# Top-k of four heads at a time, and the last gathered sum transposed later

## The chip, the cores and the metric

The kernel runs on one core of a Trainium2 chip. The time is device microseconds from the first to the last instruction of one launch, with what the launch adds around it; runs of the kernel before gave 2964.22 us in the median (2958.63 to 2974.24, three runs). The profile is of one more execution.

## The reference, cut to what matters

Two transformer blocks on 256 tokens of width 2048. The change concerns the end of the second: an expert layer with product keys, and a gate behind it.

```python
def peer(xn, w_pq, sub_k1, sub_k2, expert_u, expert_v):      # 8 heads, 128 keys a half, top 16
    q = (xn @ w_pq).reshape(B, S, 8, 2, 128)
    s1 = jnp.einsum('bshd,hnd->bshn', q[..., 0, :], sub_k1)
    s2 = jnp.einsum('bshd,hnd->bshn', q[..., 1, :], sub_k2)
    v1, i1 = lax.top_k(s1, 16)
    v2, i2 = lax.top_k(s2, 16)
    cand = (v1[..., :, None] + v2[..., None, :]).reshape(B, S, 8, 256)
    vs, ci = lax.top_k(cand, 16)
    e1 = jnp.take_along_axis(i1, ci // 16, axis=-1)
    e2 = jnp.take_along_axis(i2, ci % 16, axis=-1)
    eidx = e1 * 128 + e2                                      # one of 16384 experts
    gates = jax.nn.softmax(vs, axis=-1)
    # per token: act = gelu(expert_u[eidx] . xn);  out = sum of act * gates * expert_v[eidx]

h = h + peer(rms_norm_2(h, ffn_norm_gain), ...)
gate = jax.nn.sigmoid(rms_norm_2(h, ple_norm_gain) @ w_ple_gate)
h = h + gate * (p @ w_ple_proj)
```

## The kernel before

The program is written out by hand: each engine executes its instructions in the order in which the Python code issues them. A main line issues the projections, weight chunk by weight chunk (128 rows by 1024 numbers, 0.5 MB, four raw buffers, loaded by SyncE). Beside it run generators in *lanes*: at each new chunk `next_chunk` calls `lanes.step()`, and every lane, from lane 0 upward, goes on to its next `yield`. `until(name)` steps the lanes until a flag is set. So a generator's delay is a count of steps, not of time, and an instruction that waits holds up all that is behind it on its engine.

The expert layer has these parts.

- **Query projection** `project1`: 32 chunks of `w_pq`, 16 columns; after every second block `beside()` steps the lanes of the top-k and of the gathers once. `pq_done` copies a column from PSUM on ScalarE (L1544), `score` multiplies by the keys (L1553) and scales on ScalarE (L1555). Two columns make the scores of one head.
- **Top-k** `topk`: two lanes, even and odd heads. Per head, on two token tiles of 128: the 16 best of 128 for both halves (`top16`, L1572 to L1583), 256 candidate sums on GpSimd (L1601), the 16 best of these, the position split into two digits by six GpSimd instructions (L1606 to L1611), a comparison with 0..15 (L1616), four products on GpSimd (L1618), a sum (L1624), and the expert index on GpSimd (L1626 to L1628). The softmax of the 16 values is done in the head as well: negated maximum on GpSimd (L1612), exponential on ScalarE (L1620), reciprocal (L1625), scale (L1633).
- **First gather** `u_rows`: 256 slots (two token tiles by 128), for each an indirect DMA of one row of `w_u` per token (L1663, 128 rows of 8 KB, issued by GpSimd) and one product with sum on VectorE (L1703). Ten seats hold gathered rows for the first 128 slots, four for the rest. A seat comes free when its product is issued, and the gather waits for that product. Products begin when four heads have indices; while fewer than eight have, a product is issued every third step.
- **Weights and spots**: `weights` makes gelu times gate after products 127 and 255; `spots` builds one-hot matrices and from them, on TensorE, dense weight planes `G`.
- **Second half**: the first 1024 columns of the expert output come from 128 chunks of `w_vd` multiplied with `G` (the loop at L1878, 8 blocks a chunk, L1900), the other 1024 from 256 gathers of `w_vs` with weighted sums on VectorE (`v_rows`, L1840), two a chunk. When a tile's sum is complete it is copied (L1847) and `turned` transposes it on TensorE (L1815) and adds it to `x`: eight steps later for tile 0, at once for tile 1.
- **Gate**: after the loop the sums are added to `x` (L1904), `x_block` splits blocks 0 to 7 into high and low parts (L545, L546) and squares them for the norm (L563, L564); a narrow projection by `w_pp` follows (2 blocks deep, 16 columns, L1912), then `until("v")`, blocks 8 to 15, the norm `n5` and the gate projection of 32 chunks of `w_pg`, whose first blocks are those of rows 0 to 1023. Every chunk of `w_pp` and `w_pg` is split into a high part on ScalarE (L349) and a low part on VectorE (L350), two chunks ahead.

Of the kernel before, what the change touches and what calls it, by code (L numbers as in the profile page):

```python
# [63 lines left out]
def layout(i):  # L64
# [50 lines left out]
    a["w_pg"] = blocks(i["w_ple_gate_2"][0])  # L115
# [110 lines left out]
def program(tc, A, out, stage=99, dbg=None):  # L226
# [129 lines left out]
    lanes = Lanes(5)  # L356
    flags = {}

    def until(name):
        while not flags.get(name):  # L360
            lanes.step()
# [1169 lines left out]
    subk, qring, eg, ek, kk = cK(8, 2, 128), cK(4, T), cK(2, 128), cK(8, 2, 2, 16), cK(2, 128)  # L1531
    G.dma_start(subk.rearrange("p h s n -> p (h s n)"), A["subk"])
    sc = slab("sc").rearrange("p (t h s n) -> p t h s n", t=2, h=8, s=2)
    cT = Carve("cT")
# [51 lines left out]
    def topk(first):  # L1586

        cand, oh = cT(2, 16, 16), cT(2, 2, 16, 16)
        vv, ii, iif = cT(2, 2, 16), cT(2, 2, 16).bitcast(U32), cT(2, 2, 16)
        vs, ci, cf, c1, gs = cT(2, 16), cT(2, 16).bitcast(U32), cT(2, 16), cT(2, 2, 16), cT(2, 4)  # L1590
        xf = cT(2, 16)
        flat = lambda v: v.rearrange("p t s n -> p (t s n)")
        for h in range(first, 8, 2):
            while flags.get(("sc", h), 0) < 2:
                yield
            hs = slice(h * 16, h * 16 + 16)
            both = [(tt, s) for tt in range(2) for s in range(2)]
            yield from top16([(sc[:, tt, h, s], vv[:, tt, s], ii[:, tt, s]) for tt, s in both])
            G.tensor_copy(iif, ii)
            for tt in range(2):  # L1600
                G.tensor_add(cand[:, tt], vv[:, tt, 0][:, :, None].to_broadcast([128, 16, 16]),  # L1601
                             vv[:, tt, 1][:, None, :].to_broadcast([128, 16, 16]))
            yield
            yield from top16([(cand[:, tt].rearrange("p a b -> p (a b)"), vs[:, tt], ci[:, tt]) for tt in range(2)])

            G.tensor_copy(cf, ci)  # L1606
            G.tensor_scalar(c1[:, :, 0], cf, 1.0 / 16, -7.5 / 16, op0=OP.mult, op1=OP.add)
            G.tensor_scalar(c1[:, :, 0], c1[:, :, 0], 1.5 * 2.0 ** 23, None, op0=OP.add)
            G.tensor_scalar(c1[:, :, 0], c1[:, :, 0], 1.5 * 2.0 ** 23, None, op0=OP.subtract)
            G.tensor_scalar(c1[:, :, 1], c1[:, :, 0], -16.0, None, op0=OP.mult)  # L1610
            G.tensor_add(c1[:, :, 1], c1[:, :, 1], cf)  # L1611
            G.tensor_scalar(gs[:, :, 0], vs[:, :, 0], -1.0, None, op0=OP.mult)  # L1612
            io = iota[:, 0:16][:, None, :].to_broadcast([128, 64, 16])
            yield
            sel = oh.rearrange("p t s a b -> p (t s a) b")
            V.tensor_tensor(sel, flat(c1)[:, :, None].to_broadcast([128, 64, 16]), io, op=OP.is_equal)  # L1616
            for tt, s in both:
                G.tensor_mul(oh[:, tt, s], oh[:, tt, s], iif[:, tt, s][:, None, :].to_broadcast([128, 16, 16]))  # L1618
            for tt in range(2):
                S.activation(eg[:, tt, hs], vs[:, tt], AF.Exp, bias=gs[:, tt, 0:1], accum_out=gs[:, tt, 1:2])  # L1620
            yield
            yield
            yield
            V.tensor_reduce(flat(ek[:, h]), sel, axis=AX.X, op=OP.add)  # L1624
            V.reciprocal(gs[:, :, 2], gs[:, :, 1])  # L1625
            G.tensor_scalar(xf, ek[:, h, :, 0], 128.0, None, op0=OP.mult)  # L1626
            G.tensor_add(xf, xf, ek[:, h, :, 1])
            G.tensor_copy(idx[:, :, hs], xf)  # L1628
            flags[("idx", h)] = True
            yield  # L1630
            for tt in range(2):
                g = eg[:, tt, hs]
                G.tensor_scalar(g, g, gs[:, tt, 2:3], None, op0=OP.mult)  # L1633
            flags["heads"] = flags.get("heads", 0) + 1

    def slots_():
# [3 lines left out]
        G.tensor_copy(gate_, eg)  # L1640
# [34 lines left out]
    def u_rows():  # L1675
# [14 lines left out]
        while heads() < 4:  # L1690
            more(1)
            yield
# [115 lines left out]

    def turned(t, tt, delay):

        for _ in range(delay):
            yield
        p = pair("tok")
        for j in range(8):
            PE.transpose(p[:, j * 128:j * 128 + 128], t[:, j * 128:j * 128 + 128], ident)  # L1815
        o = xb["x"][:, 8:16, tt * 128:tt * 128 + 128]
        V.tensor_add(o, o, p.rearrange("p (k t) -> p k t", k=8))
        yield

    def v_rows():  # L1820
# [4 lines left out]
        for n in range(256):  # L1825
# [16 lines left out]
            if s == 127:  # L1842
# [5 lines left out]
                if tt:  # L1848
                    for _ in turned(t, 1, 0):
                        pass  # L1850
                else:
                    lanes.add(0, turned(t, 0, 8))
# [3 lines left out]
    lanes.add(2, topk(0))  # L1856
    lanes.add(3, topk(1))
# [5 lines left out]
    def beside():  # L1863
        for lane in (2, 3, 4):
            lanes.step_one(lane)
# [39 lines left out]
    for j in range(8):  # L1905
        x_block(j, x, C("ple"), xh, xl)
# [4 lines left out]
    def pp_done(j, ps):  # L1911
        (V.tensor_copy if j % 2 else S.copy)(pp[:, j], ps)  # L1912

    project(16, 2, (pl[:, 0], pl[:, 1]), pp_done)
    until("v")
    for j in range(8, 16):
        x_block(j, x, C("ple"), xh, xl)
# [18 lines left out]
    project(16, 16, (xh, xl), g_done, ready=lambda: flags.get("n5"))  # L1936
# [18 lines left out]
```

## Time and profile before

| | us |
|---|---|
| median of 3 runs | 2964.22 |
| the profiled execution | 2963.08 |
| its span | 2961.3 |
| TensorE busy | 2311.8 (78%) |
| VectorE busy | 1999.7 (68%) |
| ScalarE busy | 1191.2 (40%) |
| GpSimd busy | 900.9 (30%) |
| HBM read | 757.77 MB |

A busy share is an average over stages with different limits. Until about 1490 us TensorE works through dense layers; from there to 2270 the experts are chosen and gathered; then follow the second gather beside `w_vd`, to 2841, and the gate.

### The profile page before, as it was taken

To read this page: it belongs to the slowest core of one execution; us is meant where nothing else is said; L and a number is where in the kernel's file an instruction comes from. 1 tells how busy PE (TensorE), PEld (TensorE's weight loads), DVE (VectorE), ACT (ScalarE), POOL (GpSimd) and SP (SyncE) were. 2 spreads that over 40 slices of the span, in tenths; PEclk is the share of its full clock that TensorE was granted. 3 is DMA by queue.
4 is the path that set the end of the run, shared out by engine and by line. 5 is a ranking of instruction groups with operands and counts; after the bars stand their busy time and mean duration, and the time that the engine had idled before them with its cause. 6 is when DMAs were issued, how large, how long until landed. Compare 5 with 4: busy or idle time off the path is not lost.

```text
span 2961.3 us, 39499 instructions
## 1 busy us (share of the span) xinstructions
PE 2311.8 (78%) x14635; PEld 2106.1 (71%) x14635; DVE 1999.7 (68%) x2615; ACT 1191.2 (40%) x2560; POOL 900.9 (30%) x1262
## 2 busy tenths in 40 slices
PE   8999999999999999999997200022222999999799
PEld 8887898888889999998986200011122988888689
DVE  5455666555556565656537999988998866666655
ACT  4355555444444454445411000058880444400043
POOL 3202215111111000331135543333334555555420
PEclk9999999999999999999998655555555799999999
DMA  6444455655655555543557799999997799999945
GB/s 221 153 128 122 134 158 180 196 188 187 197 187 190 185 180 184 172 151 109 182 201 279 291 407 422 422 397 408 415 415 317 265 403 404 395 401 409 366 148 166
DMA packets 174675, 765.11 MB, mean 258 GB/s; under 512 B 19585, under 2 KB 22049, under 8 KB 141201
## 3 DMA queue, kind: packets, MB, share of 16 engines
q1 hardware_dynamic: 99216, 353.83, 36.0%
q0 software_dynamic: 75264, 408.75, 34.5%
q8 instruction: 115, 1.88, 0.3%
q14 instruction: 80, 0.65, 0.1%
HBM read 757.77 MB, written 4.21 MB: 257 GB/s over the span
## 4 chain that ended last, share of the span: by engine, by line
PE 59%; DMA 12%; DVE 10%; issue 9%; POOL 8%; ACT 1%; another core or an unknown queue 0%; SPq 0%; POOLq 0%; DVEq 0%; ACTq 0%
PE acc L411 11%; PE acc L1900 7%; PE acc L386 6%; PE acc L388 6%; PE acc L387 6%; DMA rows<-w_vs,idx 6%; PE acc L412 6%; POOL rows L1663 5%; DMA rows<-w_u,idx 5%; DVE rows L1703 5%; PE acc L485 3%; PE acc L483 3%; PE acc L484 3%; PE sp L1794 1%; DMA raw<-w_vd 1%
## 5 line engine op out<-in xcount | busy, mean ns | idle before, releaser
L350 DVE TENSOR_TENSOR wlo<-raw,whi 128x1024 fp32r<-128x1024 f32 (+1 forms) x501 | 613.5, 1233 | 415.1 <-ACT whi L349 408.3
L349 ACT CAST whi<-raw 128x1024 fp32r<-128x1024 f32 (+1 forms) x501 | 519.7, 1042 | 380.2 <-PE acc L387 130.9
L1703 DVE SCALAR_TENSOR_TENSOR rows<-rows,yt 128x2048 f32<-128x2048 f32 x256 | 580.3, 2285 | 42.9 <-DMA rows<-w_u,idx 38.6
L1900 PE MATMUL acc<-G,raw 128*128 128x256 f32 x2048 | 457.3, 385 | 12.4 <-DMA raw<-w_vd 11.1
L1900 PEld LDWEIGHTS acc<-G,raw 128*128 128x128 f32 x2048 | 391.8, 193 | 71.7 <-DMA raw<-w_vd 17.0
L1840 DVE SCALAR_TENSOR_TENSOR sacc<-rows,sm,sacc 128x1024 f32<-128x1024 f32 x254 | 327.3, 1289 | 143.8 <-DMA rows<-w_vs,idx 127.4
L1663 POOL DMA_INDIRECT rows<-w_u,idx x256 | 244.2, 954 | 380.0 <-DVE rows L1703 274.8
L1663 POOL DMA_INDIRECT rows<-w_vs,idx x256 | 248.8, 972 | 149.6 <-DVE sacc L1840 81.7
L411 PE MATMUL acc<-xl,whi 128*128 128x512 f32 x704 | 248.2, 391 | 0.0
L411 PE MATMUL acc<-xh,whi 128*128 128x512 f32 x704 | 248.1, 391 | 0.0
L1762 PE MATMUL sp<-P,Q 128*128 128x128 f32 x256 | 60.2, 430 | 213.9 <-ACT P L1758 213.9
L1762 PEld LDWEIGHTS sp<-P,Q 128*128 128x128 f32 x256 | 55.8, 330 | 218.6 <-ACT P L1758 218.6
L564 POOL TENSOR_TENSOR acc_sq<-acc_sq,sq 128x256 f32<-128x256 f32 x63 | 57.0, 904 | 504.6 <-ACT sq L563 502.7
L485 PE MATMUL acc<-ring,wlo 128*128 128x256 f32 x704 | 199.3, 283 | 0.1
L483 PE MATMUL acc<-ring,whi 128*128 128x256 f32 x704 | 199.3, 283 | 0.1
L484 PE MATMUL acc<-ring,whi 128*128 128x256 f32 x704 | 199.2, 283 | 0.0
L412 PE MATMUL acc<-xh,wlo 128*128 128x256 f32 x704 | 197.2, 280 | 0.0
L412 PE MATMUL acc<-xl,wlo 128*128 128x256 f32 x704 | 197.1, 280 | 0.0
L1659 PE MATMUL yt<-keep,xg 128*128 128x128 f32 x32 | 5.6, 350 | 237.6 <-DVE rows L1703 237.1
L1191 POOL TENSOR_TENSOR hT<-cF 128x256 f32<-128x256 f32 x44 | 70.8, 1609 | 372.7 <-ACT whi L349 342.8
L1659 PEld LDWEIGHTS yt<-keep,xg 128*128 128x128 f32 x32 | 5.0, 184 | 238.1 <-DVE rows L1703 237.3
L386 PE MATMUL acc<-xh,whi 128*128 128x256 f32 x520 | 150.6, 290 | 3.2 <-ACT whi L349 1.8
(486 smaller groups left out, 5692.7 us busy)
## 6 DMA issues: line engine op xcount, KB each, us to landing
raw<-w_gu SPq DMA_DIRECT2D x176, 512.0 KB
raw<-w_vd SPq DMA_DIRECT2D x128, 512.0 KB
raw<-w_down SPq DMA_DIRECT2D x88, 512.0 KB
raw<-w_out SPq DMA_DIRECT2D x32, 512.0 KB
raw<-w_pq SPq DMA_DIRECT2D x32, 512.0 KB
raw<-w_pg SPq DMA_DIRECT2D x32, 512.0 KB
raw<-w_b SPq DMA_DIRECT2D x24, 512.0 KB
raw<-w_lat SPq DMA_DIRECT2D x18, 512.0 KB
```

The lines of the kernel that those rows point to most:

```text
L349: S.copy(hi[j][:, a:b], raw[j][:, a:b])
L350: V.tensor_sub(lo[j][:, a:b], raw[j][:, a:b], hi[j][:, a:b].bitcast(F32))
L386: PE.matmul(ps, wh, xh, start=start, stop=False, **k)
L411: PE.matmul(ps, wh, xh.both(k), start=k == 0, stop=False, skip_group_check=True)
L412: PE.matmul(ps[:, :T], wl, xh[:, k], start=False, stop=k == kb - 1, skip_group_check=True)
L483: PE.matmul(o, wh, ah, start=(k == 0 and j % 2 == 0), stop=False, skip_group_check=True)
L484: PE.matmul(o, wh, al, start=False, stop=False, skip_group_check=True)
L485: PE.matmul(o, wl, ah, start=False, stop=(k == nk - 1), skip_group_check=True)
L1663: G.indirect_dma_start(dst, None, src, bass.IndirectOffsetOnAxis(ap=idx[:, tt, s:s + 1], axis=0))
L1703: V.scalar_tensor_tensor(r, r, 1.0, accT, op0=OP.mult, op1=OP.mult, accum_out=wv[:, tt, s:s + 1])
L1840: V.scalar_tensor_tensor(sacc, r, w, sacc, op0=OP.mult, op1=OP.add)
L1900: PE.matmul(o, w, gs_[k // 16][:, k % 16], start=(k == 0 and j % 2 == 0), stop=k == 127, skip_group_check=True)
```

## The change

Four lanes of top-k, each with two of the eight heads (heads n and n + 4), in place of two; a second tile `cU` for their scratch. The digits of the position by shift, mask and one conversion on VectorE; the expert index in one VectorE instruction. The candidate sums are issued ahead of the conversion of the indices. No softmax in the heads: the 16 values of each are kept in `vsa`, and `slots_` makes all gates behind the last head. Products begin at two heads in place of four. `turned` for tile 1 goes to lane 0 with a delay of 5 steps, and prepares blocks 8 to 15 a step later; blocks 0 to 7 are prepared inside the narrow projection, and the rows of `w_pg` are rolled so that the gate projection starts with blocks 8 to 15.

```diff
-    a["w_pg"] = blocks(i["w_ple_gate_2"][0])
+    a["w_pg"] = blocks(np.roll(i["w_ple_gate_2"][0], -CH, axis=0))
-    lanes = Lanes(5)
+    lanes = Lanes(7)
+    cT, cU = Carve("cT"), Carve("cU")
+    vsa = cT(8, 2, 16)
+    ga = vsa.rearrange("p h t n -> p (h t) n")
-        for h in range(first, 8, 2):
+        for h in range(first, 8, 4):
...
-            G.tensor_copy(iif, ii)
             for tt in range(2):
                 G.tensor_add(cand[:, tt], ...)
+            G.tensor_copy(iif, ii)
             yield
+            vs = vsa[:, h]
             yield from top16([(cand[:, tt].rearrange("p a b -> p (a b)"), vs[:, tt], ci[:, tt]) for tt in range(2)])
-            G.tensor_copy(cf, ci)
-            G.tensor_scalar(c1[:, :, 0], cf, 1.0 / 16, -7.5 / 16, op0=OP.mult, op1=OP.add)
-            G.tensor_scalar(c1[:, :, 0], c1[:, :, 0], 1.5 * 2.0 ** 23, None, op0=OP.add)
-            G.tensor_scalar(c1[:, :, 0], c1[:, :, 0], 1.5 * 2.0 ** 23, None, op0=OP.subtract)
-            G.tensor_scalar(c1[:, :, 1], c1[:, :, 0], -16.0, None, op0=OP.mult)
-            G.tensor_add(c1[:, :, 1], c1[:, :, 1], cf)
-            G.tensor_scalar(gs[:, :, 0], vs[:, :, 0], -1.0, None, op0=OP.mult)
+            V.tensor_scalar(cu[:, :, 0], ci, 4, None, op0=OP.logical_shift_right)
+            V.tensor_scalar(cu[:, :, 1], ci, 15, None, op0=OP.bitwise_and)
+            V.tensor_copy(c1, cu)
             io = iota[:, 0:16][:, None, :].to_broadcast([128, 64, 16])
-            yield
...
-            for tt in range(2):
-                S.activation(eg[:, tt, hs], vs[:, tt], AF.Exp, bias=gs[:, tt, 0:1], accum_out=gs[:, tt, 1:2])
             yield
             yield
             yield
             V.tensor_reduce(flat(ek[:, h]), sel, axis=AX.X, op=OP.add)
-            V.reciprocal(gs[:, :, 2], gs[:, :, 1])
-            G.tensor_scalar(xf, ek[:, h, :, 0], 128.0, None, op0=OP.mult)
-            G.tensor_add(xf, xf, ek[:, h, :, 1])
-            G.tensor_copy(idx[:, :, hs], xf)
+            V.scalar_tensor_tensor(idx[:, :, hs], ek[:, h, :, 0], 128.0, ek[:, h, :, 1], op0=OP.mult, op1=OP.add)
             flags[("idx", h)] = True
             yield
-            for tt in range(2):
-                g = eg[:, tt, hs]
-                G.tensor_scalar(g, g, gs[:, tt, 2:3], None, op0=OP.mult)
...
     def slots_():
...
-        G.tensor_copy(gate_, eg)
+        G.tensor_copy(gs, ga[:, :, 0])
+        G.tensor_tensor(ga, ga, gs[:, :, None].to_broadcast(wide), op=OP.subtract)
+        yield
+        S.activation(ga, ga, AF.Exp)
+        for _ in range(2):
+            yield
+        V.tensor_reduce(gs, ga, axis=AX.X, op=OP.add)
+        V.reciprocal(gs, gs)
+        G.tensor_mul(gate_.rearrange("p t (h n) -> p h t n", h=8), vsa, ...)
...
-        while heads() < 4:
+        while heads() < 2:
             more(1)
             yield
...
+    def finished(which):
+        for j in which:
+            part(xb["h"][:, j], xb["l"][:, j], xb["x"][:, j], C("ple", j))
+            x_square(0 if j == 8 else 1 + j % 2, xb["x"][:, j])
     def turned(t, tt, delay):
...
         V.tensor_add(o, o, p.rearrange("p (k t) -> p k t", k=8))
         yield
+        if tt:
+            finished(range(8, 16))
...
-                if tt:
-                    for _ in turned(t, 1, 0):
-                        pass
-                else:
-                    lanes.add(0, turned(t, 0, 8))
+                lanes.add(0, turned(t, tt, 5 if tt else 8))
-    lanes.add(2, topk(0))
-    lanes.add(3, topk(1))
+    for n, lane in enumerate((2, 3, 5, 6)):
+        lanes.add(lane, topk(n, cU if n > 1 else cT))
...
-        for lane in (2, 3, 4):
+        for lane in (2, 3, 5, 6, 4):
             lanes.step_one(lane)
...
-    for j in range(8):
-        x_block(j, x, C("ple"), xh, xl)
+    lanes.finish([4, 0])
...
     def pp_done(j, ps):
         (V.tensor_copy if j % 2 else S.copy)(pp[:, j], ps)
+        if j % 2:
+            finished([j // 2])
     project(16, 2, (pl[:, 0], pl[:, 1]), pp_done)
-    until("v")
-    for j in range(8, 16):
-        x_block(j, x, C("ple"), xh, xl)
...
-    project(16, 16, (xh, xl), g_done, ready=lambda: flags.get("n5"))
+    project(16, 16, (Rolled(xh), Rolled(xl)), g_done, ready=lambda: flags.get("n5"))
```

`Rolled` hands out block (k + 8) mod 16 where block k is asked for.

## Rows read from the trace of the kernel before

**Rows 1.** Stretches: from:to, length, engines' busy us (records), granted TensorE clock, DMA share, GB/s.
```profile
1563.00:1594.00 31.00, 22.84 (x103) 19.46 (x102) 18.88 (x80) 4.15 (x17) 14.09 (x36) 0.89 0.65 245
1594.00:1703.00 109.00, 43.48 (x185) 36.85 (x183) 99.76 (x257) 8.41 (x34) 55.86 (x104) 0.70 0.77 286
1790.00:1930.00 140.00, 0.00 (x0) 0.00 (x0) 130.82 (x117) 0.00 (x0) 52.45 (x56) 0.50 1.01 422
2616.00:2798.00 182.00, 173.62 (x783) 148.43 (x783) 120.52 (x95) 0.71 (x2) 97.13 (x141) 0.99 1.03 409
2798.00:2810.00 12.00, 0.62 (x4) 0.22 (x3) 6.45 (x5) 1.01 (x1) 0.74 (x4) 0.66 0.65 259
2841.40:2859.40 18.00, 13.68 (x97) 13.48 (x98) 15.23 (x22) 12.61 (x29) 5.49 (x7) 0.81 0.47 153
2859.40:2956.00 96.60, 94.67 (x776) 93.06 (x774) 62.51 (x85) 43.66 (x63) 11.14 (x23) 1.00 0.54 168
```

**Rows 2.** VectorE in order of time, products of the first gather.
```profile
1704.21 0.08 DVE L1703 DVE_READ_ACCUMULATOR rows<-rows,yt 128x1 f32 x1
...
1761.63 0.08 DVE L1703 DVE_READ_ACCUMULATOR rows<-rows,yt 128x1 f32 x1
```

**Rows 3.** Waits in 1500 to 1700: who waited for whom, us, times, longest.
```profile
ACT cK L1620 <- POOL cT L1612: 109.9, 8, 21.0
PE pa L1553 <- ACT cK L1544: 52.0, 6, 13.2
```

**Rows 4.** TensorE in order of time: start, us, instruction, idle before it.
```profile
1555.37 1.22 PE L1553 MATMUL pa<-cK 128*128 128x128 f32 x4 [6.85 <-ACT cK L1544]
```

**Rows 5.** GpSimd in order of time.
```profile
1550.67 0.95 POOL L1663 DMA_INDIRECT rows<-w_u,idx  x1 [0.30 <-issue]
...
1563.00 0.21 POOL L1628 CAST idx<-cT 128x32 int32<-128x32 f32 x1
...
1594.87 0.21 POOL L1628 CAST idx<-cT 128x32 int32<-128x32 f32 x1
...
1702.82 0.21 POOL L1628 CAST idx<-cT 128x32 int32<-128x32 f32 x1
```

**Rows 6.** VectorE's instructions by line, 1519 to 1703: count, busy us, mean ns, idle.
```profile
L1703 DVE SCALAR_TENSOR_TENSOR rows<-rows,yt 128x2048 f32<-128x2048 f32 x26 | 58.8, 2272 | 0.0
...
L1625 DVE RECIPROCAL cT<-cT 128x2 f32<-128x2 f32 x8 | 1.3, 157 | 0.0
```

**Rows 7.** All engines in order of time, around 1554.
```profile
1553.67 1.23 DVE L1616 TENSOR_TENSOR cT<-cT,keep 128x1024 f32<-128x1024 f32 x1 [4.79 <-POOL cT L1611]
...
1553.99 1.80 POOL L1663 DMA_INDIRECT rows<-w_u,idx  x1 [0.16 <-issue]
```

**Rows 8.** TensorE in order of time, end of the loop.
```profile
2787.84 10.63 PE L1900 MATMUL acc<-G,raw 128*128 128x256 f32 x48 [0.95 <-DMA raw<-w_vd]
2809.84 1.97 PE L1815 MATMUL tok<-keep,rows 128*128 128x128 f32 x8 [11.38 <-ACT rows L1847]
2811.60 29.77 PE L1900 MATMUL acc<-G,raw 128*128 128x256 f32 x128
...
2848.70 0.58 PE L386 MATMUL acc<-pl,whi 128*128 128x256 f32 x1 [4.32 <-ACT pp L1912]
```

**Rows 9.** GpSimd in order of time: a one-column copy as each chunk lands.
```profile
2806.02 0.18 POOL L1897 COPY ne<-raw 128x1 f32<-128x1 f32 x1 [2.35 <-DMA raw<-w_vd]
```

**Rows 10.** The chain of waits in order of time: start, us, what.
```profile
2858.58 0.12 PE acc L387
```

**Rows 11.** Instructions by line, 2841 to 2868.
```profile
L546 DVE SCALAR_TENSOR_TENSOR xh<-x,colt,xh 128x256 fp32r<-128x256 f32 x8 | 6.6, 887 | 0.0
L350 DVE TENSOR_TENSOR wlo<-raw,whi 128x1024 fp32r<-128x1024 f32 x5 | 6.3, 1258 | 1.3 <-ACT whi L349 1.3
...
L1912 DVE COPY pp<-acc 128x256 f32<-128x256 f32 x8 | 3.3, 416 | 1.9 <-PE acc L388 1.9
...
L1904 DVE TENSOR_TENSOR x<-x,acc 128x512 f32<-128x512 f32 x4 | 2.5, 678 | 0.0
```

More of the change, by code (lines that the diff above doesn't have):

```diff
@@ L1530, in program @@
     cK = Carve("cK")
-    subk, qring, eg, ek, kk = cK(8, 2, 128), cK(4, T), cK(2, 128), cK(8, 2, 2, 16), cK(2, 128)
+    subk, qring, ek, kk = cK(8, 2, 128), cK(4, T), cK(8, 2, 2, 16), cK(2, 128)
     G.dma_start(subk.rearrange("p h s n -> p (h s n)"), A["subk"])
     sc = slab("sc").rearrange("p (t h s n) -> p t h s n", t=2, h=8, s=2)
-    cT = Carve("cT")
+    cT, cU = Carve("cT"), Carve("cU")
+    vsa = cT(8, 2, 16)
+    ga = vsa.rearrange("p h t n -> p (h t) n")
     e1T, e2T, wT = sq[:, 0], sq[:, 1], acc_sq
@@ L1584, in top16, with topk @@
         yield
[L1586 to L1591, printed above, removed]
+    def topk(first, c):
+        cand, oh = c(2, 16, 16), c(2, 2, 16, 16)
+        vv, ii, iif = c(2, 2, 16), c(2, 2, 16).bitcast(U32), c(2, 2, 16)
+        ci, cu, c1 = c(2, 16).bitcast(U32), c(2, 2, 16).bitcast(U32), c(2, 2, 16)
         flat = lambda v: v.rearrange("p t s n -> p (t s n)")
-        for h in range(first, 8, 2):
+        for h in range(first, 8, 4):
             while flags.get(("sc", h), 0) < 2:
@@ L1639, in slots_ @@
             yield
-        G.tensor_copy(gate_, eg)
+        wide = [128, 16, 16]
+        gs = kk.rearrange("p k n -> p (k n)")[:, 0:16]
+        G.tensor_copy(gs, ga[:, :, 0])
[6 more added lines that the diff above has]
+        V.reciprocal(gs, gs)
+        G.tensor_mul(gate_.rearrange("p t (h n) -> p h t n", h=8), vsa, gs.rearrange("p (h t) -> p h t", t=2)[:, :, :, None]
+                     .to_broadcast([128, 8, 2, 16]))
         for tt in range(2):
@@ L1934, in g_done, with __init__, __getitem__ @@
         SP.dma_start(out["x"][:, j], t)
-    project(16, 16, (xh, xl), g_done, ready=lambda: flags.get("n5"))
+    class Rolled:
+        def __init__(self, x):
+            self.x = x
+        def __getitem__(self, at):
+            return self.x[(at[0], (at[1] + 8) % 16) + at[2:]]
+    project(16, 16, (Rolled(xh), Rolled(xl)), g_done, ready=lambda: flags.get("n5"))
     lanes.finish()
```

## The prediction

> **What bounds the kernel now.** I read the table of stretches first: for each engine its busy time, then the granted TensorE clock, the DMA share and GB/s. In 1790 to 1930 us the DMA share is 1.01 at 422 GB/s, in 2616 to 2798 it is 1.03 at 409 [rows 1]. One gather of `w_u` is 128 rows of 2048 floats, 1.049 MB, so at 422 GB/s it takes 2.485 us; VectorE needs 2.208 us for its product (two readings of the accumulator 26 products apart: 57.42 / 26) [rows 2]. So the gathers of `w_u`, and later those of `w_vs` beside `w_vd`, are paced by DMA, and what happens before counts by how many gathers have been served when that pace begins. Two places are not so paced. In 1563 to 1703 the DMA engines are only 0.65 and 0.77 busy, while VectorE goes from 18.9 of 31 us to 99.8 of 109: gathers wait for seats (ten), seats for products, and products stand in VectorE's queue with the top-k. In 2798 to 2841, behind the last gather, the share drops to 0.65 and TensorE does nearly nothing for 12 us.
>
> In the waits of 1500 to 1700 the longest is ScalarE's: the softmax exponential L1620 waits 109.9 us for the GpSimd chain that ends in L1612. It is in order ahead of the query copies L1544, and for those TensorE waits 52.0 us [rows 3]; one such wait is 6.85 us at 1555 [rows 4]. This looks large but is no bound by itself: from the fourth head on the order of VectorE's queue decides. Four heads' indices are written from 1594.87 to 1702.82, 27.0 us a head [rows 5], with 26 products between [rows 6], 6.5 a head or 14.4 us; top-k with its idle time takes the other 12.6, of which idle is (109 - 99.8) / 4 = 2.3 [rows 1].
>
> **Top-k and gathers: -17 us.** Four lanes alone bring little: scores arrive one head in two columns of `w_pq`, that is 2 x (8 steps from `beside` + 2 from chunks) = 20 steps, and a head takes 13, before 14. What acts is `heads() < 2` in place of 4 in `u_rows`, and that no exponential stands in the heads. A product takes three steps until all indices are flagged, so 20 / 3 = 6.7 go with each head. Counted through the steps, the products issued ahead of the eight indices are 0, 0, 5, 11, 18, 25, 31, 37; before they were 0, 0, 0, 0, 6, 13, 20, 25.
>
> The second index comes at 1563.00 now [rows 5]. In its head VectorE waits 4.79 us for the GpSimd index split behind five gathers [rows 7]; shift and mask on VectorE have no such wait, and the index no longer goes through GpSimd, which I put at 2 us: start of the products at 1556. From there VectorE has 37 x 2.208 = 81.7 us of products and six heads. A head costs 12.6 us, less the wait for the split, plus four new instructions on 32 or 64 numbers less the reciprocal. No row shows these; the reciprocal of 2 numbers takes 0.157 us [rows 6] and the comparison of 1024 numbers 1.23 us [rows 7]. I take 0.16 each, the nearer size: about 0.6 a head, and let a bit more than 1 us of idle go: 12.2. So 6 x 12.2 = 73, and the last index comes at 1556 + 82 + 73 = 1711, 8 us later than now, but with 37 products behind it. Before, at 1711, there were 26 + (1711 - 1702) / 2.208 = 30.1. The lead of 6.9 products is as many gathers issued earlier, and at DMA's pace 6.9 x 2.485 = 17 us. Bounds: with all idle gone a head is 10.9, the end 1703, the lead 10.5 and the gain 26 us; with the new instructions at 1.23 each and the idle kept it is 17.5, the end 1743, the lead -7.6 and the loss 19 us.
>
> DMA must be able to carry it: 47 gathers and some 22 weight chunks of 0.52 MB are 61 MB in 1542 to 1711, 360 GB/s, and 409 are reached elsewhere with both queues in use [rows 1]. The projection then waits for nothing that VectorE does. What GpSimd is rid of (the split, the scale of the gates, the index sum) lies beside 55.9 busy of 109 [rows 1] and gives nothing. The gates in one go cost VectorE a sum over 256 numbers and a reciprocal, once, under the 1.23 us of the comparison; they are wanted only at product 127. I count them at nothing; without that cover they would cost about 2 us. The second tile `cU` takes the tenth big buffer; the old `x` that could hold it is copied out before the projection.
>
> A gather's issue beside the comparison on VectorE takes 1.80 us, one without 0.95 [rows 5, 7]. The Trainium skill (SBUF — State Buffer, Who interferes with whom) says that copies and scalar operations on VectorE may take the port pair shared with GpSimd, which then blocks until they end. By that the new shift, mask and copy would hold up descriptors for 8 x 3 x 0.16 = 4 us, an estimate; the sum would be 4 us less if GpSimd were on the path, and the same if it is half idle, as the row says.
>
> **Last sum: -11 us.** TensorE ends a chunk at 2798.47, waits 11.38 for the copy of the last sum, transposes for 1.97 and then has 29.77 us of `w_vd`, 128 matmul passes or eight chunks of 3.72 [rows 8]. After the change the generator joins lane 0, which is stepped before lane 4, once a chunk: five empty steps, so the transposes stand ahead of the sixth chunk on, with two chunks behind them. TensorE asks for the sum at 2798.5 + 6 x 3.72 = 2820.8, and it is there at 2809.8. The weights hold: the fourth chunk on has landed by 2806.0 [rows 9], it is wanted at 2809.7, and the others need 1.3 us each at 409 GB/s. So the loop ends at 2798.5 + 29.8 + 2 = 2830.2 in place of 2841.4: 11.2. If the cover fails (fewer chunks left than six) the rest of the wait comes back; at worst all 11.
>
> **The blocks and the gate projection: -3 us.** Now blocks 0 to 7 come behind the loop, 8 to 15 behind the narrow projection; the gate projection starts 18.0 after the loop's end and takes 96.6 [rows 1], with a stall in it at the second eight. 768 passes of 0.12 [rows 10] are 92.2, so 4.4 go with the rolled order. Against that VectorE is full: 2.5 for the sums, 8 x 0.83 for the eight low parts, 8 x 0.42 copies, 4 x 1.26 weight parts, 17.4 in all [rows 11], and the sums stand behind the split of a `w_pp` chunk, which on ScalarE stands behind the blocks 8 to 15 of the last chunk: some 3 us late. TensorE's 4.32 wait for a copy [rows 8] goes, but the start stays at about 19 to 20 after the loop. 18 + 4.4 - 19.5 = 3. Bounds: +8 (start at 14.5, the narrow projection's own 96 passes, 11.5, plus 3) and -4 (start at 26, the eight in series).
>
> **Sum.** 17 + 11 + 3 = 31. The profiled execution took 2963.1 us, its span 2961.3 with 1.8 around; 2963.1 - 31 = 2932. The median of the runs is 1.1 above it: 2933.
>
> **Rivals.**
> - The early products buy nothing: gathers share DMA with `w_pq`, VectorE waits at their head with the top-k behind, and the last index comes at 1726, when 37 products would have been done before, too. For it: DMA never passed 0.77 here. Against: the waits before a product name other instructions. Lead 0; 14 us remain: 2950.
> - The tail's stall becomes a wait for VectorE: blocks and splits in series, the 3 turns to -4 and half of the 11 is lost: 17 + 1.5, 2946. For: VectorE is busy 15.2 of 18 there [rows 1].
> - More is gained: DMA has 0.35 x 31 + 0.23 x 109 = 36 us free in 1563 to 1703. If three quarters of them are used, with 18 in the tail: 2919.
> - Slower. In VectorE's queue each head's sum stands behind GpSimd's four products, and these behind gathers waiting for seats. Four heads at once make a convoy: every head's idle grows. From 16.8 us a head (6 x 16.8 + 82 = 183, the end at 1739, 43 products before against 37, -14) it eats the tail's gain; at 18 a head the end is 1746, the lead -8.8, the loss 22: 2972. Against: idle is 2.3 a head with two lanes [rows 1].
>
> **Chances.** Forecast 0.58, its own range 2922 to 2945; nothing from early products 0.14; tail lost 0.10; more 0.11; slower 0.07. The range goes from 2912, most of the larger gain, to 2956, past the case without the products. Half a per cent (15 us), about what can be told from no change, is at 2949. Below lie the forecast, the tail case, the larger gain and nearly half of the first rival, 0.83; within 0.11; slower 0.06.
>
> **What would show it.** First product at about 1556 and 37 ahead of the last index at 1705 to 1720; no query copy behind an exponential, and the projection of `w_pq` done some 35 us earlier; the last product of the expert stage 13 to 21 us earlier. The last transposes with 32 passes of `w_vd` behind them and no wait; the gate projection without idle in its first column. I am wrong if VectorE idles over 4 us a head from 1560 to 1710, if the stage's end does not follow the lead in products, or if the loop still stops for the last sum.

## The result and the profile after

The changed kernel took 2923.43 us in the median (2921.0 to 2936.61, four runs), the kernel before on the same chip 2964.85: a ratio of 0.9861, interval 0.9839 to 0.9882. A later run on another chip gave 2922.72 against 2969.46, 0.9847 (0.9824 to 0.9869). The forecast was 2933, with 31 us gained; by the ratios 41 and 45 came.

The profiled span is 2919.1 us against 2961.3. I cut both traces at four starts: of the first score, the last product with a row of `w_u`, the last product with a row of `w_vs`, the last weight load of `w_vd`.

| Stretch | Before, us | After, us | Difference | Forecast |
|---|---|---|---|---|
| to the first score | 1518.8 | 1520.9 | +2.1 | 0 |
| to the last `w_u` product | 749.1 | 727.3 | -21.8 | -17 |
| to the last `w_vs` product | 539.6 | 536.2 | -3.3 | 0 |
| to the last `w_vd` load | 33.3 | 18.4 | -14.9 | -11 |
| to the end | 120.5 | 116.2 | -4.3 | -3 |
| sum | 2961.3 | 2919.1 | -42.2 | -31 |

**Top-k.** The stretch from the first score to the last index, first in the kernel before, then in the changed one. The columns are those of [rows 1].

```profile
1518.76:1702.76 184.00, 103.72 (x460) 89.03 (x458) 143.72 (x459) 19.46 (x77) 94.22 (x184) 0.79 0.72 269
```

```profile
1520.90:1711.30 190.40, 93.20 (x460) 82.36 (x458) 173.85 (x505) 14.84 (x45) 78.44 (x104) 0.76 0.83 326
```

VectorE, the third busy time, idled for 184.00 - 143.72 = 40.3 us before and for 16.5 after, while DMA went from 269 to 326 GB/s. VectorE's waits in the two stretches, before and after (who waited for whom, us, times, longest; of the first line 14.9 us lie ahead of the first score):

```profile
DVE cT L1572 <- ACT sc L1555: 18.4, 2, 14.9
DVE cK L1624 <- POOL cT L1618: 14.0, 7, 3.7
DVE cT L1616 <- POOL cT L1611: 13.5, 5, 4.8
DVE cT L1572 <- POOL cT L1601: 8.1, 7, 3.1
```

```profile
DVE cT L1574 <- ACT sc L1557: 18.4, 2, 14.9
DVE cK L1619 <- POOL cT L1615: 5.3, 3, 3.8
DVE cK L1619 <- POOL cU L1615: 3.0, 4, 0.8
DVE cT L1574 <- POOL cT L1601: 2.9, 2, 2.1
```

The wait for GpSimd's split (13.5) is gone, that for its four products fell from 14.0 to 8.3, that for the candidate sums from 8.1 to 2.9; the wait for scores is the same. In the two stretches of [rows 1] VectorE is now all but full.

```profile
1563.00:1594.00 31.00, 31.00 (x153) 27.49 (x153) 30.13 (x84) 3.99 (x12) 13.14 (x18) 1.00 1.02 416
1594.00:1703.00 109.00, 20.11 (x100) 17.42 (x98) 104.50 (x271) 3.62 (x11) 41.42 (x54) 0.61 0.84 330
```

VectorE in order of time at the second and at the last index (L1620 writes it, L1703 is a product):

```profile
1553.15 1.22 DVE L1619 TENSOR_REDUCE cK<-cT 128x64 f32<-128x1024 f32 x1 [3.75 <-POOL cT L1615]
1554.41 0.19 DVE L1620 SCALAR_TENSOR_TENSOR idx<-cK 128x32 int32<-128x32 f32 x1
1554.52 2.28 DVE L1703 SCALAR_TENSOR_TENSOR rows<-rows,yt 128x2048 f32<-128x2048 f32 x1
...
1705.22 0.37 DVE L1608 TENSOR_SCALAR cU<-cU 128x32 uint32<-128x32 uint32 x1
1705.31 0.30 DVE L1609 TENSOR_SCALAR cU<-cU 128x32 uint32<-128x32 uint32 x1
1705.65 0.19 DVE L1610 CAST cU<-cU 128x64 f32<-128x64 uint32 x1
1705.88 1.23 DVE L1613 TENSOR_TENSOR cU<-cU,keep 128x1024 f32<-128x1024 f32 x1
...
1711.31 0.19 DVE L1620 SCALAR_TENSOR_TENSOR idx<-cK 128x32 int32<-128x32 f32 x1
1711.42 2.28 DVE L1703 SCALAR_TENSOR_TENSOR rows<-rows,yt 128x2048 f32<-128x2048 f32 x1
```

The comparison L1613 starts 0.66 us after the shift and waits for nobody; in [rows 7] it had waited 4.79 us for GpSimd. The lines of VectorE in that stretch have 37 products, 26 before [rows 6].

```profile
L1703 DVE SCALAR_TENSOR_TENSOR rows<-rows,yt 128x2048 f32<-128x2048 f32 x37 | 83.6, 2276 | 0.0
```

**Last sum.** TensorE at the end of the loop, against [rows 8]:

```profile
2760.66 35.04 PE L1903 MATMUL acc<-G,raw 128*128 128x256 f32 x160 [2.16 <-DMA raw<-w_vd]
2795.54 1.04 PE L1820 MATMUL tok<-keep,rows 128*128 128x128 f32 x8
2796.41 7.07 PE L1903 MATMUL acc<-G,raw 128*128 128x256 f32 x32
...
2807.39 0.55 PE L386 MATMUL acc<-pl,whi 128*128 128x256 f32 x1 [3.90 <-DVE x L1907]
```

The transposes have no wait, and 32 passes of `w_vd` follow them. A chunk of 16 passes takes 3.50 us (35.04 / 10), where it took 3.72 behind the stop. The stop of before had a second price, which these two rows of before (the ten microseconds behind the stop, then the rest of the loop) show in the granted clock:

```profile
2809.80:2819.80 10.00, 9.96 (x37) 8.66 (x38) 1.22 (x1) 0.00 (x0) 0.00 (x0) 0.71 0.14 39
2819.80:2841.40 21.60, 21.60 (x101) 18.79 (x101) 3.32 (x4) 2.33 (x3) 0.74 (x4) 1.00 0.58 172
```

Full is 2.4 GHz, and 0.71 a mix of that with 1.2. The transposes took 1.97 us then and 1.04 now.

### The profile page after: what moved, and what is told of

Its sections match the earlier page's. It is cut to its first block, busy times and chain, and to the rows that moved or that the text cites. A ratio compares the mean times of both kernels' runs of the same rounds, so it can differ in the third digit from the quotient of the medians.

```text
span 2919.1 us, 39399 instructions
## 1 busy us (share of the span) xinstructions
PE 2292.5 (79%) x14635; PEld 2095.4 (72%) x14635; DVE 2002.7 (69%) x2641; ACT 1185.9 (41%) x2529; POOL 874.4 (30%) x1168
## 4 chain that ended last, share of the span: by engine, by line
PE 61%; DMA 11%; issue 10%; DVE 8%; POOL 8%; ACT 1%; POOLq 0%; SPq 0%; DVEq 0%; ACTq 0%
PE acc L411 11%; PE acc L1903 8%; PE acc L386 6%; PE acc L388 6%; PE acc L387 6%; POOL rows L1663 6%; PE acc L412 6%; DMA rows<-w_vs,idx 5%; DMA rows<-w_u,idx 4%; PE acc L485 3%; PE acc L483 3%; PE acc L484 3%; DVE rows L1703 3%; PE sp L1794 1%; DMA raw<-w_vd 1%
## 5 line engine op out<-in xcount | busy, mean ns | idle before, releaser
L1703 DVE SCALAR_TENSOR_TENSOR rows<-rows,yt 128x2048 f32<-128x2048 f32 x256 | 580.0, 2284 | 40.8 <-DMA rows<-w_u,idx 36.6
L1903 PEld LDWEIGHTS acc<-G,raw 128*128 128x128 f32 x2048 | 388.1, 191 | 69.9 <-DMA raw<-w_vd 16.8
L411 PEld LDWEIGHTS acc<-xh,whi 128*128 128x128 f32 x704 | 131.7, 187 | 28.9
```

Source lines behind the costliest of these rows:

```text
L411: PE.matmul(ps, wh, xh.both(k), start=k == 0, stop=False, skip_group_check=True)
L1703: V.scalar_tensor_tensor(r, r, 1.0, accT, op0=OP.mult, op1=OP.mult, accum_out=wv[:, tt, s:s + 1])
L1903: PE.matmul(o, w, gs_[k // 16][:, k % 16], start=(k == 0 and j % 2 == 0), stop=k == 127, skip_group_check=True)
```

## The experiments

The ratios' intervals are some 6 us wide to either side, so steps below that are read from the stretches of the traces, counted from the first score on. Ratios are to the kernel before on the same chip. Names with b_ are the kernel before with one edit, those with a_ the changed kernel with one edit; a_two12 and best have two. The table (us, but for the count) holds what was read: VectorE's idle time up to the last index is the stretch's length less its busy time, as above.

| Kernel | Last index | Products ahead | VectorE idle | Last `w_u` product | Behind the last `w_vs` product | Behind the loop |
|---|---|---|---|---|---|---|
| before | 184.0 | 26 | 40.3 | 749.1 | 33.3 | 120.5 |
| changed | 190.4 | 37 | 16.5 | 727.3 | 18.4 | 116.2 |
| after_again | 190.4 | 37 | 16.5 | 725.6 | 17.6 | 116.5 |
| b_h2 | 199.6 | 38 | 30.0 | 735.6 | 33.0 | 120.2 |
| b_split | 173.4 | 25 | 25.2 | 743.5 | 32.1 | 119.8 |
| a_h4 | 167.1 | 25 | 20.0 | 733.4 | 17.5 | 116.3 |
| a_two | 192.5 | 37 | 18.4 | 731.9 | 17.6 | 117.6 |
| a_pool | 199.9 | 37 | 30.2 | 740.1 | 18.2 | 116.5 |
| a_two12 | 197.4 | 37 | 23.3 | 734.4 | 17.6 | 117.4 |
| a_pq0 | 204.7 | 44 | 15.8 | 727.6 | 18.5 | 116.5 |
| b_tail | 183.9 | 26 | 40.1 | 748.1 | 18.1 | 120.0 |
| a_d3 | 190.4 | 37 | 16.5 | 726.8 | 18.5 | 114.0 |
| a_noroll | 190.4 | 37 | 16.5 | 728.4 | 17.6 | 117.5 |
| best | 204.7 | 44 | 15.8 | 724.9 | 18.5 | 115.2 |

One rule fits all rows of these kernels: from the last index on, (256 less the products ahead) follow at 2.444 to 2.468 us each; for the kernel before (749.1 - 184.0) / 230 = 2.457. So a kernel gains by an earlier last index, or by more products ahead of it.

**The early start alone.**

```diff
 # the kernel before
-        while heads() < 4:
+        while heads() < 2:
```

> The kernel before with one edit: the first product with a gathered row waits for two heads' indices, not four. Theory: what the change saves ahead of the gathers' end is VectorE time that the products no longer need behind the last index, so the early start alone is worth most of it: the end of the products with w_u comes 12 to 15 us earlier, and the whole 2950 us (2947 to 2954). Rival 1: the early start buys nothing without the four lanes and the shorter chain of a head, since VectorE then only delays the last index by as much: 2963 to 2967. Rival 2: products ahead of the third and fourth head push the later indices back by more than they save: over 2970.

Ratio 0.9944 (0.9920 to 0.9967), 17 us less; the last product 13.5 us earlier. The theory holds, both rivals are out. 12 more products take 12 x 2.208 = 26.5 us, but the last index came only 15.6 later, because VectorE idled 10.3 us less: the products fill its waits.

```profile
1522.92:1722.52 199.60, 106.86 (x460) 91.43 (x458) 169.62 (x483) 19.48 (x77) 104.32 (x196) 0.76 0.80 306
```

**The split alone.**

```diff
 # the kernel before
-            G.tensor_copy(cf, ci)
...
-            G.tensor_add(c1[:, :, 1], c1[:, :, 1], cf)
+            V.tensor_scalar(cu[:, :, 0], ci, 4, None, op0=OP.logical_shift_right)
+            V.tensor_scalar(cu[:, :, 1], ci, 15, None, op0=OP.bitwise_and)
+            V.tensor_copy(c1, cu)
...
-            yield
...
-            G.tensor_scalar(xf, ek[:, h, :, 0], 128.0, None, op0=OP.mult)
-            G.tensor_add(xf, xf, ek[:, h, :, 1])
-            G.tensor_copy(idx[:, :, hs], xf)
+            V.scalar_tensor_tensor(idx[:, :, hs], ek[:, h, :, 0], 128.0, ek[:, h, :, 1], op0=OP.mult, op1=OP.add)
```

> The kernel before with one edit: shift, mask and copy on VectorE give the index halves, and one operation on VectorE the index; two lanes, four heads ahead of the first product and the exponential in each head stay. Theory, from what the last runs showed (the split back on GpSimd cost the four lanes 13 us from the first score on): a head's chain loses seven GpSimd operations in a row, the waits of VectorE for them (13.5 us for the split) go, and the indices come earlier: 8 to 14 us less, 2951 to 2957. Rival: the split matters only where four lanes share GpSimd, and two lanes hide it: 0 to 4 us less, 2961 to 2965.

Ratio 0.9960 (0.9941 to 0.9978), 12 us; the last product 5.6 us earlier. The whole lies in the expected range, with an interval of 7 to 18 us; the stage, where the theory puts the gain, gave less than the 8 expected, and the trace's span is 7.2 us shorter in all. Idle fell by 15.1 us, more than with any other edit of the kernel before. Two of the waits above are left up to the last index:

```profile
DVE cK L1620 <- POOL cT L1614: 12.9, 7, 3.9
DVE cT L1572 <- POOL cT L1601: 7.0, 7, 2.9
```

The wait for the split is gone, the other two stay. The last index came 10.6 us sooner with one product fewer ahead of it (2.5 us); the other 2.5 went in the pace behind it, 2.468 against 2.457.

**The changed kernel with each part taken back.** Three kernels: four heads ahead of the first product, two lanes, and the split on GpSimd.

```diff
 # a_h4
-        while heads() < 2:
+        while heads() < 4:
 # a_two
-        for h in range(first, 8, 4):
+        for h in range(first, 8, 2):
...
-    for n, lane in enumerate((2, 3, 5, 6)):
+    for n, lane in enumerate((2, 3)):
 # a_pool
-            V.tensor_scalar(cu[:, :, 0], ci, 4, None, op0=OP.logical_shift_right)
...
+            G.tensor_copy(cf, ci)
...
+            G.tensor_add(c1[:, :, 1], c1[:, :, 1], cf)
+            yield
```

> The changed kernel with one edit: the first product waits for four heads again. Theory: about six products fewer stand ahead of the last index, part of which the four lanes have already filled with work; the products with w_u end 6 to 8 us later than in the changed kernel: 2930 us (2928 to 2933). Rival: the four lanes and the short chain alone give the gain, the early start is idle: 2922 to 2925. Other rival: the early start is all of it, and without it the stage is as long as before: 2941 to 2944.

> The changed kernel with two heads side by side in place of four (shift and mask on VectorE, gates behind the last head and the early start kept). Theory: VectorE is full in this stage either way, so two lanes are nearly enough once the chain of a head has no hop to GpSimd for its split: the products with w_u end 1 to 3 us later, 2925 us (2923 to 2928). Rival: four lanes are what fills VectorE, and with two it idles behind GpSimd's multiplications in each head: 8 heads by at least 1.5 us, 2935 us and over.

> The changed kernel with the split of the candidate's index back on GpSimd (six operations in place of shift, mask and copy on VectorE; the sum of index parts stays on VectorE). Theory: with four lanes GpSimd's six operations lie beside other lanes' VectorE work, but the first indices, and with them the first gathers and products, come later: 5 to 8 us lost, 2930 us (2927 to 2932). Rival: the split's place is worth nothing with four lanes, or a little gain since VectorE sheds three operations a head (8 by about 0.7 us): 2918 to 2924. Other rival: the split was the main thing, and the stage goes back to its old length: over 2938.

Ratios 0.9895 (0.9870 to 0.9920), 0.9858 (0.9835 to 0.9882), 0.9909 (0.9888 to 0.9930). Against 727.0, the mean of the four traces in which this stage is that of the changed kernel (725.6 to 728.4, after_again, a_d3 and a_noroll among them), the last product came 6.4, 4.9 and 13.1 us later. The first stage is as expected, though the median, 2935.40, lies above the range given for the whole. Two lanes cost nothing in the ratio; of the 4.9 us in the stage, where 1 to 3 were expected, 2.1 are a later index and the rest is pace. The rival that four lanes are essential is out: idle is 18.4 against 16.5. The third missed: 13.1 where 5 to 8 were expected, and the median, 2942.53, is that of the second rival. Its reason holds by half: the stage is 740.1, between 727 and 749. With the split on GpSimd four lanes idle as long (30.2) as two do (30.0 in b_h2), and both have the last index at 200.

```profile
1531.23:1731.13 199.90, 93.20 (x460) 82.36 (x458) 169.71 (x481) 14.90 (x45) 94.56 (x152) 0.74 0.80 310
```

**The changed kernel again, and the scatter.**

> The changed kernel itself once more, as a base for the others of this call. The profiles of the four kernels run before differ by up to 12 us in when their first score is ready (1518.8 to 1531.2), with nothing changed ahead of it; so stages are now measured from the first score on. Theory: from the first score to the end of the products with w_u the changed kernel needs 730 us, within 2, whichever chip it runs on, and the whole is 41 us (37 to 45) under the kernel before. Rival: the small VectorE operations, which were 7 to 9 per cent longer in all four kernels run before (310 against 283 ns for the last index search), belong to the chip: then it needs 733 to 736 us where they are long.

Up to the last index the two traces agree: 190.4 us, 37 products, idle 16.5. The stage is 725.6, where 728 to 732 were expected, and the ratio gives 45 us, at the upper end: the theory holds for the part up to the last index, and the rest varies by more than 2 us. The rival is not met here, for the searches of this trace are recorded at 0.28 us; the long ones are all in b_h2, a_h4, a_two and a_pool. There they cost no more: up to the last index VectorE was busy for 174.1 us in a_two and for 173.9 in the changed kernel, with 37 products in both. In the changed kernel's trace and in a_two's, two searches in a row:

```profile
1558.10 0.28 DVE L1577 FIND_INDEX8 cU<-cU,sc 128x8 uint32<-128x128 f32 x1
...
1558.36 0.28 DVE L1577 FIND_INDEX8 cU<-cU,sc 128x8 uint32<-128x128 f32 x1
```

```profile
1698.26 0.32 DVE L1585 FIND_INDEX8 cT<-cT,sc 128x8 uint32<-128x128 f32 x1
...
1698.52 0.32 DVE L1585 FIND_INDEX8 cT<-cT,sc 128x8 uint32<-128x128 f32 x1
```

They start 0.26 us apart in both: the records overlap, so starts and busy time are to be compared, not durations.

**More seats, and more products ahead.** Two lanes with the spare slab as two seats more; and one step of the lanes per product once the query projection is done.

```diff
 # a_two12 (on a_two)
-    rows_ = [slab("rows%d" % j).rearrange("p (n d) -> p n d", n=2) for j in range(5)]
+    rows_ = [slab("rows%d" % j).rearrange("p (n d) -> p n d", n=2) for j in range(5)] + [cU.t.rearrange("p (n d) -> p n d", n=2)]
...
-    seat = [n % 10 if n < 128 else n % 4 for n in range(256)]
+    seat = [n % 12 if n < 128 else n % 4 for n in range(256)]
 # a_pq0
-            for _ in range(2 if heads() < 8 else 0):
+            for _ in range(2 if heads() < 8 and not flags.get("pq") else 0):
```

> The changed kernel with two heads side by side, and the slab of the two other lanes as two more places for gathered rows (12 in place of 10). Theory: what is left to gain in the gathers is transfer time: DMA moved 244 to 315 GB/s in 1640 to 1720 beside 420 elsewhere, since all ten places were full while VectorE was with the indices; two more places let two more gathers of 2.5 us go ahead: 3 to 5 us less than the changed kernel with two lanes, and 0 to 4 us less than the changed kernel: 2920 to 2924 where that is 2924. Rival: VectorE's own time for 256 products and the indices sets the end, and more places buy nothing: 2924 to 2929.

> The changed kernel with one step of the heads' lanes per product in place of three once the projection with w_pq is done, so that some 85 products stand ahead of the last index in place of 37. Theory: VectorE is full until the last index and DMA (2.485 us a row set at 422 GB/s against VectorE's 2.37) sets the pace behind it, so each product moved ahead of the last index is worth only that difference: 48 by 0.1, 4 to 5 us less; the last index comes 100 to 120 us later. Rival 1: what counts is the number of rows gathered by then, and DMA's unused time in 1640 to 1720 (some 30 us) comes back: 15 us and more. Rival 2: products wait for rows in VectorE's order ahead of the indices, nothing or a loss of up to 5 us.

Ratios 0.9869 (0.9847 to 0.9892) and 0.9868 (0.9847 to 0.9888). Seats bought nothing, the rival's case, though the median, 2932.43, lies above both ranges: VectorE idled 4.9 us more than with two lanes and ten seats, and the last index came 4.9 later. The waits tell where: VectorE waited 9.4 us for the candidate sums, 4.6 in a_two, so GpSimd made them later. In a_pq0 only 44 products stood ahead of the last index; 85 had been expected, so its theory was not put to the test. The seven more moved that index by 14.3 us, 2.05 each, and the last product by nothing that can be told (727.6 against 727.0). No wait of VectorE for a row lies ahead of the last index, so rival 2 has no support either. What both runs show is that DMA's unused time in the middle of the stage was not got back this way: VectorE, not DMA, is full there.

**The tail alone.**

```diff
 # the kernel before
-                if tt:
-                    for _ in turned(t, 1, 0):
-                        pass
-                else:
-                    lanes.add(0, turned(t, 0, 8))
+                lanes.add(0, turned(t, tt, 5 if tt else 8))
...
+    lanes.finish([4, 0])
...
-    until("v")
```

> The kernel before with one edit: the last gathered sum's transposes are issued five chunks on, and the finishing of x blocks 8 to 15 stays where it was, behind the projection with w_pp. Theory: TensorE's stop of 11.4 us goes and with it the lower granted clock that followed it: the loop with w_vd ends 15 us earlier, the rest keeps its 120 us: 2950 (2947 to 2953). Rival: without the finishing moved ahead, VectorE's waits behind the loop take it back: 2956 to 2962.

Ratio 0.9959 (0.9941 to 0.9978), 12 us. The median, 2958.28, lies in the rival's range, but the kernel before took 2969.46 on this chip, some 5 us more than where the ranges were set. The trace decides: the stretch to the loop's end is 15.2 us shorter and the rest is 120.0, against 120.5. The theory holds; TensorE in order of time:

```profile
2798.27 32.09 PE L1896 MATMUL acc<-G,raw 128*128 128x256 f32 x144 [0.27 <-DMA raw<-w_vd]
2830.19 1.04 PE L1815 MATMUL tok<-keep,rows 128*128 128x128 f32 x8
2831.06 7.07 PE L1896 MATMUL acc<-G,raw 128*128 128x256 f32 x32
```

**Behind the loop.** The transposes three chunks on, and `w_pg` in its old order.

```diff
 # a_d3
-                lanes.add(0, turned(t, tt, 5 if tt else 8))
+                lanes.add(0, turned(t, tt, 3 if tt else 8))
 # a_noroll
-    a["w_pg"] = blocks(np.roll(i["w_ple_gate_2"][0], -CH, axis=0))
+    a["w_pg"] = blocks(i["w_ple_gate_2"][0])
...
-    project(16, 16, (Rolled(xh), Rolled(xl)), g_done, ready=lambda: flags.get("n5"))
+    project(16, 16, (xh, xl), g_done, ready=lambda: flags.get("n5"))
```

> The changed kernel with the last gathered sum's transposes three chunks on in place of five. Theory: the transposes then stand at the copy's end plus about 2.7 us and still wait for nothing; the finishing of x blocks 8 to 15 on VectorE and GpSimd ends 7 us earlier and is out of the way of w_pp's first chunk and of the adds behind the loop; TensorE's wait of 3.9 us ahead of the projection with w_pp falls to 1.0 to 1.5: from the loop's end to the end of the span 113 us in place of 115.8, the whole 2 to 3 us less (2920 where the changed kernel has 2923). Rival: the transposes come too early and TensorE stops for the copy again, with the lower clock behind it: 3 us and more lost.

> The changed kernel with the chunks of w_pg in their old order (the gate projection goes through x blocks 0 to 15, not 8 to 15 first). Theory: the blocks 0 to 7 are finished between the results of the projection with w_pp, block 7 at 2821.0 us in the changed kernel, and the gate projection wants its eighth block 2.5 us after it starts at about 2819.5: the order is worth 0 to 1 us. Rival: TensorE stops for the blocks one after the other, 0.9 us each: 4 to 7 us lost from the loop's end to the end of the span.

Ratios 0.9854 (0.9832 to 0.9877) and 0.9888 (0.9871 to 0.9906). With three chunks the stretch behind the loop is 114.0, 2.2 to 2.5 less, as expected in size; but the wait itself fell only to 2.92, not to 1.0 to 1.5.

```profile
2816.28 0.36 PE L386 MATMUL acc<-pl,whi 128*128 128x256 f32 x1 [2.92 <-DVE x L1907]
```

The other 1.3 to 1.5 us are clock. The 2.7 us behind the wait, in the changed kernel (wait 3.90) and in a_d3 (2.92):

```profile
2807.40:2810.10 2.70, 2.70 (x13) 2.70 (x14) 2.70 (x4) 1.05 (x3) 0.00 (x0) 0.50 0.80 299
```

```profile
2816.20:2818.90 2.70, 2.62 (x22) 2.65 (x23) 2.70 (x4) 1.28 (x4) 0.46 (x1) 1.00 0.83 266
```

At 0.50, which is 1.2 GHz, TensorE began 13 passes, at 1.00, 2.4 GHz, 22. That part of the gain was luck: best has the same edit and a shorter wait (2.63), the clock was low behind it for part of the time, and 115.2 us came, 1.1 to 1.3 less than in the changed kernel.

Without the rolled order no wait of TensorE is added (its waits behind the loop are the same 3.9 and 0.2 us); 117.5 is 1.1 to 1.3 more. That is clock again, not the order: a_two and a_two12, which keep the order, have 117.6 and 117.4. Behind the loop in best, then in a_noroll, where the low clock lasted longer:

```profile
2819.30:2822.00 2.70, 2.65 (x17) 2.68 (x18) 2.70 (x4) 1.08 (x3) 0.50 (x1) 0.75 0.82 259
```

```profile
2817.10:2823.90 6.80, 5.81 (x27) 5.84 (x28) 5.04 (x9) 2.68 (x7) 1.39 (x3) 0.50 0.68 230
```

The theory holds: the order is worth nothing that these traces show. The 8 to 12 us by which its ratio lies above the changed kernel's are in no stretch that the edit touches; its trace has 9 of them ahead of the first score.

**Both edits.** The one line of a_d3 and the one of a_pq0.

> The changed kernel with both edits, the transposes three chunks on and one step of the lanes per product behind the projection with w_pq. Theory: 4.5 and 2.5 us less than the changed kernel, 2916 where that is 2923. Rival: either is nothing, and the other alone is left; or the later indices delay the gates' and slots' work behind the first 128 products, and the time is over 2925.

2920.42 us, ratio 0.9846 (0.9828 to 0.9864), against 0.9861 and 0.9847 of the changed kernel: not told apart from it, and 4 us over what was expected. Its trace has 1.1 to 1.3 us less behind the loop, and the last `w_u` product at 724.9, 0.7 under the least of the four traces above.

## Why the prediction was right, step by step

- *First product, count and last index.* 1554.5, 37 and 1711.3 against 1556, 37 and 1711. The size of the term was short, -21.8 against -17, for two reasons. I took 30.1 products as done before at 1711; the trace of before has 29 ended there and one begun at 1710.84: 0.9 x 2.46 = 2.2. And the stage began 2.1 us later in the execution profiled after, which equal clock times hide. From the second index on VectorE idled 6.3 us, 1.0 in each of six heads, against some 1.3 in the forecast.
- *What acts.* I named the early start and the missing exponential. The early start is confirmed (b_h2, a_h4), and that four lanes alone bring little (a_two). The exponential was not tried by itself, but the runs speak against it. The last score came 144 to 172 us after the first in every kernel with the exponential in the heads, and 94 to 95 in every kernel without it. The last index did not follow: 199.6 in b_h2 with the last score at 171.5, 199.9 in a_pool with the last score at 94.0. VectorE's wait for scores is 18.4 us with and without it. So the 109.9 us of ScalarE [rows 3] were indeed no bound; they held up the projection, whose last matmul came 46.6 us earlier, against 35 forecast.
- *What the forecast left out.* Idle up to the last index fell by 23.8 us. I let 4.79 go for the split in the second head [rows 7], and a bit over 1 us in each of six. By the waits above the split is 13.5 of it, the wait for products 5.7 and that for the candidate sums 5.2, which I did not name. The split was under-rated: taken back it cost 13.1. The order of the candidate sums was not tried alone. In b_split and a_h4, both with the split on VectorE and 25 products ahead, VectorE waited 7.0 and 2.1 us for them, and the last index came 6.3 us sooner in the second; the two kernels also differ by the lanes and the exponential. The parts don't add: the split is worth 5.6 alone and 13.1 taken back, the early start 13.5 and 6.4.
- *The new instructions.* Less 2.208 a product, VectorE's busy time went from 143.7 - 57.4 = 86.3 to 173.9 - 81.7 = 92.2, 0.7 a head, against the 0.6 taken.
- *GpSimd's port.* The 256 issues of `w_u` gathers take 936, 943 and 1068 ns (least, median, most), so the delay of 4 us, which I estimated by the Trainium skill (SBUF — State Buffer, Who interferes with whom) for shift, mask and copy, is not in this trace. Three issues lie beside a shift and a mask and took no longer. Nor was an issue beside the comparison held up:

```profile
1546.90 0.94 POOL L1663 DMA_INDIRECT rows<-w_u,idx  x1 [0.30 <-issue]
1547.55 0.29 DVE L1608 TENSOR_SCALAR cT<-cT 128x32 uint32<-128x32 uint32 x1
...
1548.12 1.28 DVE L1613 TENSOR_TENSOR cT<-cT,keep 128x1024 f32<-128x1024 f32 x1
1548.15 0.95 POOL L1663 DMA_INDIRECT rows<-w_u,idx  x1 [0.30 <-issue]
```

  So the 1.80 of [rows 7] is not the price of every issue beside a comparison. In the four kernels whose comparison waits for GpSimd's split (before, b_h2, b_tail, a_pool) all twelve issues that began 0.12 to 0.43 us into a comparison took 1.71 to 2.02 us. In the ten others the issues beside one began within 0.11 us of its start or at least 1.13 us into it, and took 0.95 at most. Why the start matters is open.
- *Last sum.* The order came out as forecast. The term was mis-sized, 14.9 against 11.2, by what the low clock behind the stop had cost: eight chunks of 3.72 in place of 3.50 are 1.8, the transposes 0.9. With the wait of 11.4 that is 14.1. Of the last 0.8, 0.7 is the loop's lead over the gathers: with 128 passes left, the last `w_vs` product was still 9.0 us away before and 9.7 after.
- *Blocks and gate projection.* -4.3 against -3. The adds were late as forecast (TensorE waited 3.90), but the gate projection started 16.8 us after the loop (2820.23 against 2803.48), not 19.5. It took 93.6 us, in a_noroll 93.6 as well: what paid is that the blocks were finished earlier, not the rolled order to which I gave the 4.4. Blocks 8 to 15 inside the loop and 0 to 7 inside the narrow projection were not tried apart. The total is also uncertain by the clock: kernels that are the same behind the loop have 116.2 to 117.6 there.
- *Rivals.* "Early products buy nothing" fell with b_h2. "The tail's stall becomes a wait for VectorE" did not come true: TensorE waits 3.90 us for VectorE behind the loop, but its wait of 4.32 [rows 8] is gone, and the term came out at -4.3. "More is gained" was nearest in sign, but not by its reason: DMA's free time in the middle was not for sale (a_two12, a_pq0). The convoy of four heads did not show; its nearest case, a_pool, idles as long as two lanes do.

That the `w_vs` stretch is 3.3 us shorter was not tested; over all traces it lies between 536.2 and 540.1, whatever the edit.

## What to carry to other kernels

Where an in-order engine is nearly full, add up its idle time up to the point from which another resource sets the pace, and count the useful work ahead of that point: these two numbers gave every kernel here to some 3 us. A hop to another engine for a few tiny instructions can cost the waiting engine more than doing them itself: 13.5 us in eight heads, 4.79 in the worst, against 0.66 a head. What a part is worth depends on the others, so try it both alone and taken back. A stop of TensorE is to be priced with the lower clock behind it, and that clock differs between executions of one kernel, so a step of a microsecond there needs more than one trace.

## What the hardware showed that was not expected

The time of the first score fell into two groups, 1518.8 to 1522.9 and 1530.1 to 1535.6 us (eight and six of the traces above), with nothing changed ahead of it. Most of the difference comes from one stage. Its matmuls of 128 by 512 in the changed kernel and in a_d3 (count, ns least, median and most, first and last start):

```profile
L411 PE MATMUL acc<-xl,whi x704: 391/391/476, 465.1 to 952.3; 128*128 128x512 f32 x176
```

```profile
L411 PE MATMUL acc<-xl,whi x704: 392/398/476, 467.0 to 962.5; 128*128 128x512 f32 x176
```

487.2 us against 495.5, at a granted clock of 1.00 in both (600 to 900 us). All six late traces have a median of 398 or 399 ns there, the others 391 to 395. Why is open. It is larger than several of the steps measured here, and it is the reason for counting from the first score.
